# Two-part SwiGLU input products in 512 columns, a new order of the mixers' pieces, and other loads and final norm

## The chip, the cores and the metric

The kernel runs on one core of a Trainium2 chip. The core has a matrix engine (TensorE; PE in the profile, PEld for its loading of weights), VectorE (DVE), ScalarE (ACT), GpSimd (POOL) and a queue engine (SP) that here only issues DMAs. Sixteen DMA engines move data between the chip's memory (HBM) and the core's own (SBUF); TensorE writes into PSUM, eight banks of 512 four-byte columns in each of 128 partitions. The metric is the device time of one execution in microseconds (us).

## What is computed

The reference is an encoder of two layers over 256 tokens of 1024 channels in float32. Each layer adds half a SwiGLU, a mixer of three kinds of heads, and half a second SwiGLU; a norm ends it.

```python
def rms_norm(x, g):
    xf = x.astype(jnp.float32)
    y = xf * lax.rsqrt(jnp.mean(xf * xf, axis=-1, keepdims=True) + EPS)
    return (y * g.astype(jnp.float32)).astype(x.dtype)

def swiglu(h, w_in, w_out):
    gate, up = jnp.split(h @ w_in, 2, axis=-1)
    return (jax.nn.silu(gate) * up) @ w_out
...
    for l in range(DEPTH):
        lam_init = 0.8 - 0.6 * math.exp(-0.3 * l)
        x = x + 0.5 * swiglu(rms_norm(x, ln_ffn1[l]), ffn1_w_in[l], ffn1_w_out[l])
        h = rms_norm(x, ln_mix[l])
        x = x + hybrid_mixer(h, w_mix_in[l], conv_w[l], sink_logits[l], diff_lambda[l],
                             diff_norm_g[l], dn_A_log[l], dn_dt_bias[l], dn_norm_g[l],
                             w_mix_out[l], lam_init)
        x = x + 0.5 * swiglu(rms_norm(x, ln_ffn2[l]), ffn2_w_in[l], ffn2_w_out[l])
    return rms_norm(x, ln_final)
```

The hidden width of SwiGLU is 2752. The mixer projects 1024 channels to windowed attention (6 heads), differential attention (4 heads) and a gated delta rule (6 heads, forward and backward, in chunks of 64 tokens, with a short convolution ahead of it and a triangular inverse for each chunk), and projects the joined heads back.

## The kernel before

**Layout.** x stays in SBUF through the whole kernel with channels on the partitions: `x[128, 8, 256]`, eight blocks k of 128 channels by 256 tokens. Weights come from HBM once, in tiles of 128x1024 (512 KB), through a ring of eight raw tiles `wr` (L255).

**Two-part products.** The SwiGLUs and the mixer's last projection split both operands into a high part, rounded to the matrix engine's fast four-byte type, and the rest. `load` (L257 on) writes the high part `wh` of a weight tile on ACT (L264) and the low part `wl` on DVE (L265); `prep` does the same for x times the norm's gain, giving `xh` (L243) and `xl` (L244). `mm3` (L270 to L272) then adds three products: high by high, high weight by low x, low weight by high x. Each is one weight load of 128x128 and one pass of 256 columns.

**SwiGLU** (`ffn`). The input stage runs over 21 blocks j of 128 hidden channels and a tail of 64. Gate and up of a block are 2 x 8 groups of `mm3`, and share one PSUM bank, 256 columns each (block 0 has two banks). `hidden` then multiplies the gate by the norm's factor `rb` (L288, DVE), takes its silu (L289, ACT), multiplies it by up (L291, DVE), and splits it into `hh` and `hl` (L293, ACT; L294, DVE). The output stage runs over 8 blocks d of output channels, 21 groups of `mm3` and a tail each, and adds to x on DVE (L360, L361). The norm's factor is computed after block 1 (`norm_scale`): sums of squares by products with a column of ones (L211), the root on DVE or ACT, and a product that spreads it over the partitions (L220).

**Start** (`start`). SP issues four loads of x, each followed by a quarter of the two weight tiles of block 0 (`ar`); ACT issues `cols`, the gains and conv weights. Block 0 runs as pieces arrive.

**Mixer** (`mixer`). Some 150 pieces (projections, conv taps, scores, softmaxes, rows of the inverse, scan steps, output products) are issued in the order of the string `ORDER`. A piece may be: `c` a conv channel block, `co` its silu and transposition, `p` an attention projection, `d` and `w` scores of a differential or windowed head, `h` and `hw` their outputs, `ir`, `im`, `io` parts of the inverse, `sa`, `sb`, `sc` parts of a scan step, `z` a gate projection, `o` an output product. `BANK` names the PSUM pool of each kind of product: `pm` has two banks, `pd` four, `pt` two. `SHARED` lists pieces of work that go to another engine than their usual one: `t` a conv tap through ACT and POOL, `g` a slope added by a matrix product instead of DVE (L710), `S` and `O` parts of the scan on POOL instead of DVE (L1033, L1046), `x` a residual addition on ACT and POOL (L1079, L1080), `s` a part of silu on POOL.

The Tile framework turns the program into one fixed instruction stream for each engine, and may move an instruction ahead of one that it expects to wait; the order of the program gives the priorities.

**End** (`final`). The final norm's factor stays in PSUM; eight DVE instructions (L1129) multiply x, gain and factor, 256 columns each, and four DMAs on two queues write pairs of blocks.

Of the kernel before, what the change touches and what calls it, by code (L numbers as in the profile page):

```python
# [56 lines left out]
class Kernel:  # L57
    def __init__(self, ctx, tc, ins, out):
# [12 lines left out]
        self.x = self.xp.tile([P, KD, S], F32, tag="x", name="x")  # L71
        self.col = cp.tile([P, 150], F32, name="col")
# [3 lines left out]
        warm = cp.tile([P, 1], F32, name="warm")  # L76
        nc.scalar.activation(warm, self.onec, AF.Copy)

    def start(self, gcol, pool=None, src=None):

        nc = self.nc
        n = KD // 2
        self.ahead = []
        if pool is not None:
            for j in range(2):
                w, go = self.fetch(src, j * 1024, 1024, n, pool)
                h = pool.tile([P, 1024], F32R, name=f"ah{j}")
                lo = pool.tile([P, 1024], F32R, name=f"al{j}")
                self.ahead.append((w, go, h, lo))
        for i in range(n):  # L90
            nc.sync.dma_start(self.x[:, 2 * i : 2 * i + 2, :], self.ins["x"][:, 2 * i : 2 * i + 2, :])
            for w, go, h, lo in self.ahead:
                go[i]()
            if i == 0:
                nc.scalar.dma_start(self.col, self.ins["cols"])
        for i in range(n):
            for k in (2 * i, 2 * i + 1):
                self.prep(k, gcol, False)
            c = slice(i * 256, i * 256 + 256)
            for w, go, h, lo in self.ahead:  # L100
                nc.scalar.activation(h[:, c], w[:, c], AF.Copy)
                nc.vector.tensor_tensor(lo[:, c], w[:, c], h[:, c].bitcast(F32), ALU.subtract)
        self.ahead = [a[2:] for a in self.ahead]
# [99 lines left out]

    def norm_scale(self, name, last=False, log=True):

        nc = self.nc
        ps = self.psum([P, 512], f"{name}_ps", "pt")
        for p in range(2):
            parts = [t for t in (self.sq, self.sq7) if t is not None]
            for t in parts:  # L210
                nc.tensor.matmul(  # L211
                    ps[:, p : p + 1], lhsT=t[:, p * P : (p + 1) * P], rhs=self.onec, start=t is parts[0], stop=t is parts[-1]
                )
        v = self.sp.tile([P, 2], F32, tag="nv", name=f"{name}_v")
# [52 lines left out]

    def mm3(self, out, ah, al, bh, bl, start, stop):
# [6 lines left out]
    def ffn(self, l, i, gnext, first, late=False):  # L275
# [3 lines left out]
        with tc.tile_pool(name=f"hp{nm}", bufs=1) as hp, tc.tile_pool(name=f"ht{nm}", bufs=3) as ht:  # L279
# [3 lines left out]

            def hidden(j, gate, up, rows, base):
                t = ht.tile([P, S], F32, tag="t", name="t")
                s = ht.tile([P, S], F32, tag="s", name="s")
                h = ht.tile([P, S], F32, tag="h", name="h")
                nc.vector.tensor_tensor(t[:rows], gate, rb[:rows], ALU.mult)  # L288
                nc.scalar.activation(s[:rows], t[:rows], AF.Silu)  # L289
# [57 lines left out]
            for d in range(KD):  # L347
# [940 lines left out]
```

## Time and profile before

| | us |
|---|---|
| median of 3 runs | 1120.86 (1120.8 to 1122.6) |
| the profiled execution's own time | 1121.32 |
| its span, first to last instruction | 1119.5 |
| mean granted TensorE clock, share of full | 0.991 |

The profile shows one execution. An instruction's row gives its line, engine, operation, output and inputs, shape and count. "Busy" is the time in which an engine has an instruction under way; matrix products overlap each other, so their mean duration (283 ns for 256 columns) is longer than the step from one to the next. "Idle before" names what ended an engine's wait. The stages, by their instructions: SwiGLU to 197 us, mixer to about 355, SwiGLUs to 747, the second mixer to 904, SwiGLU to 1109, final norm. A few per cent of the matrix products can be missing from such a record.

### The profile page before, as it was taken

To read this page: it belongs to the slowest core of one execution; us is meant where nothing else is said; L and a number is where in the kernel's file an instruction comes from. 1 tells how busy PE (TensorE), PEld (TensorE's weight loads), DVE (VectorE), ACT (ScalarE), POOL (GpSimd) and SP (SyncE) were. 2 spreads that over 40 slices of the span, in tenths; PEclk is the share of its full clock that TensorE was granted. 3 is DMA by queue.
4 is the path that set the end of the run, shared out by engine and by line. 5 is a ranking of instruction groups with operands and counts; after the bars stand their busy time and mean duration, and the time that the engine had idled before them with its cause. 6 is when DMAs were issued, how large, how long until landed. Compare 5 with 4: busy or idle time off the path is not lost.

```text
span 1119.5 us, 22207 instructions
## 1 busy us (share of the span) xinstructions
PE 1077.2 (96%) x9098; PEld 1009.7 (90%) x9098; DVE 751.0 (67%) x1374; ACT 545.4 (49%) x1006; POOL 60.1 (5%) x109
## 2 busy tenths in 40 slices
PE   7999999999799999999999999999989999999996
PEld 7999999777568999999999999988756789999996
DVE  7766654579958866666566666536897697666643
ACT  6544433263773654544444454423648455445441
POOL 0000001100101000000000000121010010000010
PEclk9999999999899999999999999999989999999998
DMA  9655654422322555565555565534223135555521
GB/s 331 225 182 187 199 178 136 132 94 95 113 96 77 165 174 189 182 200 184 171 174 184 188 197 182 170 115 150 85 85 132 42 130 172 189 183 195 187 95 38
DMA packets 49637, 173.65 MB, mean 155 GB/s; under 512 B 5504, under 2 KB 6784, under 8 KB 49536
## 3 DMA queue, kind: packets, MB, share of 16 engines
q1 hardware_dynamic: 49104, 171.64, 46.2%
q8 instruction: 71, 1.16, 0.4%
q10 hardware_dynamic: 432, 0.60, 0.2%
q14 instruction: 30, 0.25, 0.1%
HBM read 171.17 MB, written 1.05 MB: 154 GB/s over the span
## 4 chain that ended last, share of the span: by engine, by line
PE 78%; DVE 13%; ACT 4%; issue 3%; DMA 1%; POOL 1%; DVEq 0%; SPq 0%; ACTq 0%
PE ps L272 21%; PE ps L270 21%; PE ps L271 21%; PE pj L455 4%; PE pv L466 2%; DVE pr L825 2%; DVE wl L265 2%; PE py L270 1%; DVE pp L826 1%; PE py L271 1%; PE py L272 1%; DVE pad L568 1%; ACT wh L264 1%; DVE mxd L740 1%; PE px L995 1%
## 5 line engine op out<-in xcount | busy, mean ns | idle before, releaser
L265 DVE TENSOR_TENSOR wl<-wr,wh 128x1024 fp32r<-128x1024 f32 x270 | 330.5, 1226 | 167.6 <-ACT wh L264 167.1
L264 ACT ACTIVATE wh<-wr 128x1024 fp32r<-128x1024 f32 x270 | 284.2, 1054 | 243.9 <-issue 153.0
L270 PE MATMUL ps<-xh,wh 128*128 128x256 f32 x1336 | 378.6, 283 | 0.6 <-ACT wh L264 0.6
L272 PE MATMUL ps<-xh,wl 128*128 128x256 f32 x1336 | 378.3, 283 | 0.8 <-DVE wl L265 0.8
L271 PE MATMUL ps<-xl,wh 128*128 128x256 f32 x1336 | 377.9, 283 | 0.0
L272 PEld LDWEIGHTS ps<-xh,wl 128*128 128x128 f32 x1336 | 256.3, 192 | 1.2 <-DVE wl L265 1.2
L270 PEld LDWEIGHTS ps<-xh,wh 128*128 128x128 f32 x1336 | 256.3, 192 | 0.8 <-ACT wh L264 0.8
L271 PEld LDWEIGHTS ps<-xl,wh 128*128 128x128 f32 x1336 | 256.3, 192 | 0.0
L270 PE MATMUL ps<-hh,wh 128*128 128x256 f32 x672 | 190.2, 283 | 0.0
L271 PE MATMUL ps<-hl,wh 128*128 128x256 f32 x672 | 190.2, 283 | 0.0
L272 PE MATMUL ps<-hh,wl 128*128 128x256 f32 x672 | 190.2, 283 | 0.0
L455 PE MATMUL pj<-xf,wr 128*128 128x256 f32 x544 | 128.8, 387 | 1.2 <-DVE dqk L686 1.2
L270 PEld LDWEIGHTS ps<-hh,wh 128*128 128x128 f32 x672 | 129.0, 192 | 0.0
L271 PEld LDWEIGHTS ps<-hl,wh 128*128 128x128 f32 x672 | 129.0, 192 | 0.0
L272 PEld LDWEIGHTS ps<-hh,wl 128*128 128x128 f32 x672 | 129.0, 192 | 0.0
L455 PEld LDWEIGHTS pj<-xf,wr 128*128 128x128 f32 x544 | 101.7, 193 | 18.3 <-issue 3.9
L293 ACT ACTIVATE hh<-h 128x256 fp32r<-128x256 f32 x88 | 36.1, 416 | 90.3 <-DVE h L291 90.3
L198 POOL TENSOR_TENSOR sqacc<-sqacc,sqt 128x256 f32<-128x256 f32 x27 | 24.5, 907 | 741.6 <-ACT sqt L194 741.6
L288 DVE TENSOR_TENSOR t<-ps,f_rb 128x256 f32<-128x256 f32 x88 | 36.9, 424 | 38.0 <-PE ps L272 37.7
L294 DVE TENSOR_TENSOR hl<-h,hh 128x256 fp32r<-128x256 f32 x88 | 36.8, 423 | 30.4 <-ACT hh L293 30.4
L194 ACT ACTIVATE sqt<-x 128x256 f32<-128x256 f32 x49 | 19.8, 409 | 56.3 <-DVE x L361 52.5
L568 DVE SCALAR_TENSOR_TENSOR pad<-pad,cwh 128x256 f32<-128x256 f32 x68 | 33.1, 487 | 12.1 <-ACT pad L562 6.8
(319 smaller groups left out, 1212.7 us busy)
## 6 DMA issues: line engine op xcount, KB each, us to landing
wr<-in_ffn SPq DMA_DIRECT2D x258, 512.0 KB, 3.4
wr<-in_mix SPq DMA_DIRECT2D x50, 512.0 KB, 3.4
wr<-in_mix SPq DMA_DIRECT2D x8, 408.0 KB, 3.1
wr<-in_mix SPq DMA_DIRECT2D x8, 384.0 KB, 2.9
x<-in_x SPq DMA_DIRECT2D x4, 256.0 KB, 4.1
ar<-in_ffn SPq DMA_DIRECT2D x8, 128.0 KB, 4.2
cb<-in_constb SPq DMA_DIRECT2D x1, 588.0 KB, 10.2
out_y<-fo SPq DMA_DIRECT2D x2, 256.0 KB, 2.4
```

The source lines that it names most:

```text
L198: (eng or nc.gpsimd).tensor_tensor(self.sq, self.sq, t, ALU.add)
L264: nc.scalar.activation(h, w, AF.Copy)
L265: nc.vector.tensor_tensor(lo, w, h.bitcast(F32), ALU.subtract)
L270: mm(out, lhsT=ah, rhs=bh, start=start, stop=False)
L271: mm(out, lhsT=ah, rhs=bl, start=False, stop=False)
L272: mm(out, lhsT=al, rhs=bh, start=False, stop=stop)
L288: nc.vector.tensor_tensor(t[:rows], gate, rb[:rows], ALU.mult)
L293: nc.scalar.activation(hh[:n, j, :], h[:n], AF.Copy)
L294: nc.vector.tensor_tensor(hl[:n, j, :], h[:n], hh[:n, j, :].bitcast(F32), ALU.subtract)
L455: mm(ps[:, 0:S], lhsT=w[:, k * P : (k + 1) * P], rhs=xf[:, k, :], start=k == 0, stop=k == KD - 1)
L466: mm(st[name][p][:, 0:n], lhsT=xf[:, k, p * P : (p + 1) * P], rhs=w[:, c], start=k == 0, stop=k == KD - 1)
L568: stt(cv, pad[:, w : w + S], cw[:, i * 5 + w : i * 5 + w + 1], cv, ALU.mult, ALU.add)
```

## The change

Five things change together.

1. In the input stage of SwiGLU, high and low part of x stand side by side in a tile `x2` (`[128, 2, 256]` for each k). `mm2` multiplies the high weight by both at once, 512 columns into a whole PSUM bank, and the low weight by the high part, 256 columns into the bank's first half. `halves` copies the second half out (ACT) and adds the first (DVE). Gate and up have a bank each in every block. The output stage and the mixer keep `mm3`. In block 0 the weights are packed so that the first tile holds k 0 to 3 of gate and up.
2. At the start, x and `cols` lie in one array that ACT's queue loads in three pieces; the weights of block 0 go over SP in two pieces and one whole tile; six products of zeros run on PE before.
3. The order of the mixers' pieces, some PSUM pools and some of the sharing between engines are others.
4. In the final norm, x times the gain is written by ACT during the last output stage (`xg`); DVE multiplies by the factor in four instructions of 512 columns.
5. Around the last norm's sums, twice three products without use (`idle_mm`) run on PE.

```diff
-lt A:0 A:1 A:2 K N A:3 G V c:1:0 c:1:1 c:0:0 c:0:2 c:1:2 clear GS co:1:0 c:0:1 co:1:1 co:1:2 ce:1 GE GT E:1 qn:1
-co:0:0 co:0:1 co:0:2 ce:0 qn:0 qc:1:1 E:0 E:3 qc:1:0 c:2:0 c:2:1 E:2 qc:0:0 qc:0:1 ic X:0:0 X:1:1 X:0:1 X:1:0 i ir:1:2
-ir:2:3 ir:3:4 ir:4:5 ir:5:6 p:15 ir:6:7 ir:7:8 im:0 im:1 im:2 c:2:2 p:14 p:13 co:2:0 p:16 d:0 d:2 co:2:1 co:2:2 im:3
...
+lt K A:0 A:1 clear A:2 N A:3 V c:0:0 c:1:0 c:1:1 c:1:2 G c:0:2 co:1:0 co:1:1 c:0:1 co:1:2 co:0:0 c:2:1 GS ce:1 GT qn:1
+qc:1:0 GE co:0:1 co:0:2 E:1 ce:0 qn:0 qc:0:1 E:0 qc:0:0 qc:1:1 E:3 ic X:0:0 X:0:1 c:2:0 E:2 X:1:1 X:1:0 i ir:1:2
+ir:2:3 ir:3:4 p:14 ir:4:5 ir:5:6 ir:6:7 ir:7:8 p:15 im:0 p:13 im:1 co:2:0 im:2 p:16 im:3 co:2:1 c:2:2 d:2 d:1 p:12
...
-    pj="pm", pv="pd", pz="pm", py="pm", pss="pd", pg="pt", pgr="pd", ptr="pd", pkq="pt", pe="pd", pq="pd", p1="pd",
-    p2="pt", pk="pd", px="pt", pS="pt", po="pd", pw="pt", pT="pd", pso="pd", pto="pd",
+    pj="pm", pv="pd", pz="pm", py="pm", pss="pd", pg="pt", pgr="pd", ptr="pd", pkq="pt", pe="pd", pq="pt", p1="pt",
+    p2="pt", pk="pd", px="pt", pS="pt", po="pt", pw="pt", pT="pd", pso="pt", pto="pt",
...
-SHARED = set("O2 d0 d1 d2 d3 g5 s3 t1 t8 x4 x5 x6".split())
+SHARED = set("O3 S1 d0 d1 d2 d3 g2 g5 s4 t0 t3 t8 x0 x4 x6 x7".split())
...
+            zero = pool.tile([P, S], F32, name="zero")
+            nc.vector.memset(zero, 0.0)
+            wm = self.psum([P, 512], "wm", "pt")
+            for i in range(NWARM):
+                nc.tensor.matmul(wm[:, 0:S], lhsT=zero[:, 0:P], rhs=zero, start=True, stop=True)
             for j in range(2):
-                w, go = self.fetch(src, j * 1024, 1024, n, pool)
+                w, g = self.fetch(src, j * 1024, 1024, 2 - j, pool)
+                go += g
...
-        for i in range(n):
-            nc.sync.dma_start(self.x[:, 2 * i : 2 * i + 2, :], self.ins["x"][:, 2 * i : 2 * i + 2, :])
-            for w, go, h, lo in self.ahead:
-                go[i]()
-            if i == 0:
-                nc.scalar.dma_start(self.col, self.ins["cols"])
+        cuts = [0] + [NCOL + 512 * i for i in (1, 2, 4)]
+        for a, b in zip(cuts, cuts[1:]):
+            nc.scalar.dma_start(self.xc[:, a:b], self.ins["x"][:, a:b])
+        warm = self.cp.tile([P, 1], F32, name="warm")
+        nc.scalar.activation(warm, self.onec, AF.Copy)
+        for g in go:
+            g()
...
+    def mm2(self, bank, ah, al, b, start, stop):
+
+        mm = self.nc.tensor.matmul
+        mm(bank, lhsT=ah, rhs=b.rearrange("p a t -> p (a t)"), start=start, stop=False)
+        mm(bank[:, 0:S], lhsT=al, rhs=b[:, 0, :], start=False, stop=stop)
...
+            def halves(ps, tag):
+
+                u = ht.tile([P, S], F32, tag=tag, name=tag)
+                nc.scalar.activation(u, ps[:, S : 2 * S], AF.Copy)
+                nc.vector.tensor_tensor(u, u, ps[:, 0:S], ALU.add)
+                return u
...
-                nc.vector.tensor_tensor(t[:rows], gate, rb[:rows], ALU.mult)
-                nc.scalar.activation(s[:rows], t[:rows], AF.Silu)
+                nc.vector.tensor_tensor(gate, gate, rb[:rows], ALU.mult)
+                nc.scalar.activation(s[:rows], gate, AF.Silu)
...
-                ps = self.psum([P, 512], "ps", "pm" if j % 3 == 0 else "pd")
-                pu = self.psum([P, 512], "pu") if j == 0 else ps
+                ps, pu = (self.psum([P, 512], t, "pm" if j % 3 == 0 else "pd") for t in ("ps", "pu"))
...
-                    self.mm3(o, w[g][0][:, c], w[g][1][:, c], self.xh[:, k, :], self.xl[:, k, :], k == 0, k == KD - 1)
+
+                    n, q = (k // 4, k // 2 % 2 * 4 + g * 2 + k % 2) if j == 0 else (g, k)
+                    c = slice(q * P, (q + 1) * P)
+                    self.mm2((ps, pu)[g], w[n][0][:, c], w[n][1][:, c], self.x2[k], k == 0, k == KD - 1)
...
-                        hidden(j_, pg[:, 0:S], pu[:, S : 2 * S], P, (0,))
+                        hidden(j_, halves(pg, "t"), halves(pu, "u"), P, (0,))
...
                 if gnext is None:
                     self.sq_add(d, last=d == KD - 1)
+                    if d == 0:
+                        self.xg = self.xp.tile([P, KD, S], F32, tag="xh", name="xg")
+                    nc.scalar.activation(self.xg[:, d, :], self.x[:, d, :], AF.Copy, scale=self.col[:, 48 + d : 49 + d])
...
-        for k in range(KD):
-            nc.vector.scalar_tensor_tensor(o[:, k, :], self.x[:, k, :], self.col[:, 48 + k : 49 + k], rb, ALU.mult, ALU.mult)
-            if k % 2:
-                (nc.sync, nc.scalar)[k // 2 % 2].dma_start(self.out[:, k - 1 : k + 1, :], o[:, k - 1 : k + 1, :])
+        for i in range(KD // 2):
+            k = slice(2 * i, 2 * i + 2)
+            nc.vector.tensor_tensor(o[:, k, :], self.xg[:, k, :], rb.unsqueeze(1).to_broadcast([P, 2, S]), ALU.mult)
+            (nc.sync, nc.scalar)[i % 2].dma_start(self.out[:, k, :], o[:, k, :])
```

`idle_mm(3)` runs the products of 256 columns with the identity as weight, once ahead of the sums of the last norm and once behind them.

More of the change, by code (lines that the diff above doesn't have):

```diff
@@ L32 @@
 NROW = 158
+NCOL = 150
+NWARM = 6
 C_U0, C_U1, C_ONE, C_ID, C_MM = 0, 128, 256, 384, 512
@@ L70, in __init__ @@
         cp = self.cp
-        self.x = self.xp.tile([P, KD, S], F32, tag="x", name="x")
-        self.col = cp.tile([P, 150], F32, name="col")
+        self.xc = self.xp.tile([P, NCOL + KD * S], F32, tag="x", name="x")
+        self.col = self.xc[:, 0:NCOL]
+        self.x = self.xc[:, NCOL:].rearrange("p (k t) -> p k t", k=KD)
         self.cst = None
@@ L98, in start @@
                 self.prep(k, gcol, False)
-            c = slice(i * 256, i * 256 + 256)
-            for w, go, h, lo in self.ahead:
+            if self.ahead:
+                w, h, lo = self.ahead[i // 2]
+                c = slice(i % 2 * 512, i % 2 * 512 + 512)
                 nc.scalar.activation(h[:, c], w[:, c], AF.Copy)
                 nc.vector.tensor_tensor(lo[:, c], w[:, c], h[:, c].bitcast(F32), ALU.subtract)
-        self.ahead = [a[2:] for a in self.ahead]
+        self.ahead = [a[1:] for a in self.ahead]
     def constants(self):
@@ L202, in log_table, with idle_mm @@
         self.tc.keep_in_program_order(self.nc.scalar.preload_act_table_set("natural_log_exp_and_others"))
+    def idle_mm(self, n, tag="pm"):
+        ps = self.psum([P, 512], "idle", tag)
+        for i in range(n):
+            self.nc.tensor.matmul(ps[:, 0:S], lhsT=self.ident, rhs=self.cst[:, C_U0 : C_U0 + S], start=True, stop=True)
     def norm_scale(self, name, last=False, log=True):
         nc = self.nc
+        if last:
+            self.idle_mm(3)
         ps = self.psum([P, 512], f"{name}_ps", "pt")
@@ L213, in norm_scale @@
                 )
+        if last:
+            self.idle_mm(3)
         v = self.sp.tile([P, 2], F32, tag="nv", name=f"{name}_v")
@@ L239, in prep @@
         if k == 0:
-            self.xh = self.xp.tile([P, KD, S], F32R, tag="xh", name="xh")
-            self.xl = self.xp.tile([P, KD, S], F32R, tag="xl", name="xl")
+            self.x2 = []
+        if k % 4 == 0:
+            x2 = self.xp.tile([P, KD // 2, 2, S], F32R, tag=("xh", "xl")[k // 4], name="x2")
+            self.x2 += [x2[:, i] for i in range(KD // 2)]
         g = self.col[:, gcol + k : gcol + k + 1]
-        nc.scalar.activation(self.xh[:, k, :], self.x[:, k, :], AF.Copy, scale=g)
+        nc.scalar.activation(self.x2[k][:, 0, :], self.x[:, k, :], AF.Copy, scale=g)
         nc.vector.scalar_tensor_tensor(
-            self.xl[:, k, :], self.x[:, k, :], g, self.xh[:, k, :].bitcast(F32), ALU.mult, ALU.subtract
+            self.x2[k][:, 1, :], self.x[:, k, :], g, self.x2[k][:, 0, :].bitcast(F32), ALU.mult, ALU.subtract
         )
@@ L331, in ffn @@
                 c = slice(k * P, (k + 1) * P)
-                self.mm3(ps[:, 0:S], wh[:, c], wl[:, c], self.xh[:, k, :], self.xl[:, k, :], k == 0, k == KD - 1)
-            hidden(NF, ps[0:TAIL, 0:S], ps[TAIL : 2 * TAIL, 0:S], TAIL, (0, TAIL))
+                self.mm2(ps, wh[:, c], wl[:, c], self.x2[k], k == 0, k == KD - 1)
+            t = halves(ps, "t")
+            up = ht.tile([P, S], F32, tag="u", name="up")
+            nc.scalar.activation(up[:TAIL], t[TAIL : 2 * TAIL], AF.Copy)
+            hidden(NF, t[:TAIL], up[:TAIL], TAIL, (0, TAIL))
             if gnext is None:
@@ L1254, in pack @@
     gh = np.stack([np.tile(f[n][l], 2) for l in range(DEPTH) for n in ("diff_norm_g", "dn_norm_g")], axis=1)
-    out["cols"] = np.concatenate([g.transpose(2, 0, 1).reshape(P, 56), cw, gh], axis=1)
+    cols = np.concatenate([g.transpose(2, 0, 1).reshape(P, 56), cw, gh], axis=1)
+    out["x"] = np.concatenate([cols, out["x"].reshape(P, KD * S)], axis=1)
     rows = [
```

21 lines of the change are left out of this document (10 added, 11 removed).

## The prediction

> **What bounds the kernel now.** I read the page first: engine shares, then the chain that ended last.
>
> ```profile
> span 1119.5 us, 22207 instructions
> PE 1077.2 (96%) x9098; PEld 1009.7 (90%) x9098; DVE 751.0 (67%) x1374; ACT 545.4 (49%) x1006; POOL 60.1 (5%) x109
> PE ps L272 21%; PE ps L270 21%; PE ps L271 21%; PE pj L455 4%; PE pv L466 2%; DVE pr L825 2%; DVE wl L265 2%; PE py L270 1%; DVE pp L826 1%; PE py L271 1%; PE py L272 1%; DVE pad L568 1%; ACT wh L264 1%; DVE mxd L740 1%; PE px L995 1%
> ```
>
> TensorE is the bound, and 63% of the chain is the three products of SwiGLU. Next, the windows by stage (columns: length, then busy time and count of PE, PEld, DVE, ACT, POOL, clock, DMA):
>
> ```profile
> 0.00:5.80 5.80, 0.00 (x0) 0.00 (x0) 1.19 (x8) 2.69 (x6) 0.51 (x12) 1.00 0.61 187
> 5.80:13.80 8.00, 7.94 (x48) 7.88 (x48) 7.40 (x21) 7.19 (x22) 0.00 (x0) 1.00 0.97 316
> 13.80:30.00 16.20, 14.77 (x118) 14.04 (x117) 14.36 (x36) 9.54 (x10) 0.00 (x0) 1.00 1.02 400
> 58.00:138.00 80.00, 80.00 (x669) 80.00 (x668) 52.13 (x73) 39.04 (x58) 0.00 (x0) 1.00 0.58 191
> 197.50:355.00 157.50, 146.59 (x1307) 114.43 (x1307) 122.20 (x294) 84.97 (x226) 15.31 (x29) 0.98 0.31 101
> 746.70:904.00 157.30, 146.70 (x1306) 114.41 (x1306) 121.93 (x293) 84.78 (x226) 15.24 (x29) 0.98 0.31 101
> ```
>
> In the SwiGLU stage PE has no gap: 669 products in 80.0 us, 119.6 ns each. A mixer leaves PE idle for 157.5 - 146.6 = 10.9 us. So the first question is what sets the 119.6 ns.
>
> **SwiGLU input.** Three products of 256 columns become one of 512 and one of 256: weight loads fall from three to two, columns stay at 768. The count is 4 x (21 x 16 + 8) = 1376 groups; the page shows 1336 under one name, the rest have other tile names. What a group costs depends on which of the two, columns or loads, sets the pace. These rows (start, duration; the last one is a tile's minimum, median, maximum in ns) separate them:
>
> ```profile
> 7.22 0.41 PE L272 MATMUL pu<-xh,al 128*128 128x256 f32 x1
> 9.35 0.41 PE L270 MATMUL pu<-xh,ah 128*128 128x256 f32 x1
> 209.69 17.28 PE pj L455 x80
> 266.41 0.59 PE L732 MATMUL pss<-ddb,sdiag 128*128 128x512 bf16 x2
> L732 PE MATMUL pss<-ddb,sdiag x16: 379/379/379, 266.4 to 828.2; 128*128 128x512 bf16 x16
> 300.18 1.10 PE L784 MATMUL pso<-V,PT 128*128 128x64 f32 x8
> L784 PE MATMUL pso<-V,PT x64: 275/275/323, 293.3 to 858.4; 128*128 128x64 f32 x64
> ```
>
> In the slow first microseconds the same products stand 10 steps apart over 2.13 us: 213 ns. [...] A product of only 64 columns with a four-byte 128x128 weight still takes (1.10 - 0.275) / 7 = 118 ns. So about 118 to 120 ns is the floor of a **weight load**, whatever is streamed. Two bf16 products of 512 columns take 0.59, one 0.379: 211 ns. [...] So I price the 512-column product at 216 and the 256-column one behind it at 120 ns: 336 for 360, **24 ns a group, 1376 x 24 = 33.0 us**. [...]
>
> [...]
>
> What the halves cost: per block of 128 hidden channels, two ACT copies out of PSUM and two DVE additions. From the stage's groups (58 to 138 us; the third column is idle time before them):
>
> ```profile
> L265 DVE TENSOR_TENSOR wl<-wr,wh 128x1024 fp32r<-128x1024 f32 x28 | 34.3, 1225 | 14.4 <-ACT wh L264 14.4
> L264 ACT ACTIVATE wh<-wr 128x1024 fp32r<-128x1024 f32 x28 | 29.4, 1051 | 22.1 <-issue 22.1
> L288 DVE TENSOR_TENSOR t<-ps,f_rb 128x256 f32<-128x256 f32 x14 | 6.0, 425 | 7.2 <-PE ps L272 7.2
> L294 DVE TENSOR_TENSOR hl<-h,hh 128x256 fp32r<-128x256 f32 x14 | 5.9, 424 | 5.8 <-ACT hh L293 5.8
> L293 ACT ACTIVATE hh<-h 128x256 fp32r<-128x256 f32 x14 | 5.8, 417 | 17.6 <-DVE h L291 17.6
> L291 DVE TENSOR_TENSOR h<-s,ps 128x256 f32<-128x256 f32 x14 | 5.8, 415 | 0.0
> L289 ACT ACTIVATE s<-t 128x256 f32<-128x256 f32 x14 | 5.6, 399 | 0.0
> L1079 ACT ACTIVATE xt<-py x6: 363/377/384, 355.3 to 909.0; 128x256 f32<-128x256 f32 x6
> ```
>
> DVE per block: 2 x 1.225 + 0.425 + 0.415 + 0.424 = 3.71 us, plus 2 x 0.42 = 4.55. ACT: 2 x 1.051 + 0.399 + 0.417 = 2.92, plus 2 x 0.377 = 3.67. The block itself goes from 16 x 0.36 = 5.76 to 16 x 0.336 = 5.38. Both fit, so I cost them at **0**; DVE stands at 85% then. Each block takes two PSUM banks instead of one, so three blocks are in flight; at the start block 3 waits for block 0's banks, but the halves are read out before the norm's factor is known. The weight stream rises from 191 to some 205 GB/s, far under the 400 that the start shows: 0. The new packing of block 0 asks for the second tile earlier; in later SwiGLUs both are loaded ahead: 0.
>
> **Start.** Loads go out on two queues, weights in 3 pieces instead of 8, and six zero products run before the data.
>
> ```profile
> 0.73 0.42 ACTq L95 DMA_DIRECT2D col<-in_cols  x1
> 1.18 1.28 ACT L77 ACT_TABLE_LOAD   x1 [1.18 <-PEq L1276]
> 5.86 0.58 PE L270 MATMUL ps<-xh,ah 128*128 128x256 f32 x1 [5.86 <-ACT ah L101]
> 10.03 0.42 ACT L101 ACTIVATE ah<-ar 128x256 fp32r<-128x256 f32 x1 [0.48 <-DMA ar<-in_ffn]
> 14.61 0.38 PE L270 MATMUL ps<-xh,wh 128*128 128x256 f32 x1 [0.61 <-ACT wh L264]
> 15.87 0.39 PE L272 MATMUL ps<-xh,wl 128*128 128x256 f32 x1 [0.76 <-DVE wl L265]
> ```
>
> Block 0 waits for its last piece of weights at 10.0 us, and its first 20-odd products run at 213 instead of 120 ns: 2 us. Earlier pieces and a warm array are worth 0 to 3 us together. What follows is close to DMA and DVE (1.02 and 14.36 of 16.2 us busy), where the additions go too, so I take **2 us**. On ACT's queue three loads of x now stand ahead of the table load: 3 x 0.42 + 1.28 from 0.73 us on ends at 3.3, before the first product at 5.9, so 0. [...]
>
> **Mixers.** The pieces are the same; their order, some PSUM pools and the sharing between engines differ. Two windows, one wait in the timeline, and the prices of what changes engine (L1033: minimum, median, maximum):
>
> ```profile
> 270.00:285.00 15.00, 10.44 (x56) 7.47 (x56) 14.93 (x21) 8.44 (x29) 2.54 (x2) 0.95 0.22 71
> 285.00:300.00 15.00, 12.60 (x64) 10.15 (x64) 13.98 (x22) 9.00 (x22) 3.55 (x2) 0.82 0.45 141
> 286.21 2.17 PE L699 MATMUL pss<-wq 64*128 64x256 f32 x8 [5.77 <-DVE c L748]
> 294.99 0.69 DVE L710 SCALAR_TENSOR_TENSOR sc<-wd,pss 128x512 f32<-128x512 bf16 x1 [0.35 <-PE pT L436]
> L1033 DVE TENSOR_TENSOR Stmp<-SC,egl x6: 551/554/557, 333.0 to 888.1; 64x384 f32<-64x384 f32 x4, 128x384 f32<-128x384 f32 x2
> L568 DVE SCALAR_TENSOR_TENSOR pad<-pad,cwh 128x256 f32<-128x256 f32 x68 | 33.1, 487 | 12.1 <-ACT pad L562 6.8 <-POOL pad L566 3.1 <-POOL pad L552 0.3
> 343.25 1.02 POOL L1046 TENSOR_TENSOR O<-O,SC 128x384 f32<-128x384 f32 x1 [44.53 <-DVE SC L1044]
> ```
>
> Most of PE's idle time lies between 270 and 300 us, where DVE runs the inverse and is 96% busy; one PE wait there is 5.77 us. DVE is relieved of one slope addition (0.69), one conv tap net (0.49), the scaling of the state in scan step 1 (2 x 0.55) and one residual addition (0.42): 2.7 us, of which only the slope stands near the full stage. POOL takes those at about 1 us each and has time; the two state halves end before the product that they meet, so 0. Five tiles move from a pool of four banks to one of two, and may make products wait. What the new order is worth isn't visible in a trace of the old one: at best the idle 10.9 us, at worst another wait of the size of that 5.77. I take 2 us a mixer, near the relief: **4 us**, bounds +22 and -12.
>
> **End.** Multiplying by the gain moves into the last stage; then come 4 products of 512 columns instead of 8 of 256.
>
> ```profile
> 1110.13 0.38 PE L211 MATMUL fin_ps<-onec,sqt 128*128 128x1 f32 x2 [1.37 <-ACT sqt L194]
> 1112.27 0.71 PE L220 MATMUL fin_pb<-cst,fin_r 128*128 128x128 f32 x4 [1.31 <-DVE fin_r L182]
> 1113.02 3.22 DVE L1129 SCALAR_TENSOR_TENSOR fo<-x,col,fin_pb 128x256 f32<-128x256 f32 x8 [0.81 <-PE fin_pb L220]
> ```
>
> A 512-element DVE pass is 0.69: about 2.5 for 3.22, **0.7 us**. The idle products, 3 x 0.216 us, fit into PE's 1.37 and 1.31 us waits; uncovered they would cost 0.65 each. The added ACT pass lies beside the norm chain: 0.
>
> **Sum.** The profiled execution took 1121.3 us (span 1119.5 and 1.8 around it). 1121.3 - 33.0 - 2.0 - 4.0 - 0.7 = 1081.6; the median of the runs, 1120.9, lies 0.4 lower: **1081 us**.
>
> **Rivals.**
> [...]
> - *Columns set the pace.* No gain from the groups: 1121.3 - 6.7 = 1114.6, less than 0.6% faster. [...]
> - *DVE becomes the bound, slower.* Its waits for ACT in the stage were (14.4 + 5.8) / 14 = 1.44 us a block. If in the new fixed order none of them hides behind other work, a block takes 4.55 + 1.44 = 5.99 us, 0.23 more than 5.76: 84 blocks x 0.23 = 19 us, 1121.3 + 19 - 6.7 = 1134. It costs from 5.38 us a block on and makes the kernel slower from 5.76 + 6.7 / 84 = 5.84. Against it: DVE can run ahead by two pairs of weight tiles, and waits shrink when it is late.
>
> **Chances.** Forecast 0.70, exchange cost 0.13, columns 0.07, DVE 0.10 (0.07 of it beyond the break-even). A measurement of this kernel can tell about 0.2% from no change. Faster: 0.70 + 0.13 + 0.06 + 0.02 = 0.91; same 0.02; slower 0.07. The range 1066 to 1100 takes in the forecast with the mixers 15 us better or 12 worse, and the exchange cost, about 0.8.
>
> **What would show it.** In the stage's windows PE without gaps and 16 groups in 5.38 us, the 512-column products 216 ns from the next, the others 120 (227 and 120 for the exchange cost, 240 and 120 for columns); DVE near 85% and idle only on PE. Wrong if PE shows idle time for DVE or ACT in the SwiGLU stage, if a mixer is longer than 157 us, or if block 1 does not start before 14.6 us.

## The result, and the profile after

The changed kernel takes **1111.6 us** (median of 4 runs, 1110.03 to 1112.02), the kernel before 1121.62 beside it. The ratio is 0.9905, 95% interval 0.9893 to 0.9917: faster by 10 us, 0.95%, where 40 us were forecast. The profiled execution took 1112.02 us; the sum of the prediction, 1081.6, is 30.4 us below it.

From the page of the changed kernel: its span, TensorE's share, and the chain that ended last by line.

```profile
span 1110.2 us, 19882 instructions
PE 1074.5 (97%) x7746; PEld 937.5 (84%) x7748; DVE 797.4 (72%) x1529; ACT 597.9 (54%) x1190; POOL 70.0 (6%) x117
PE ps L296 15%; PE pu L296 14%; PE ps L297 7%; PE pu L297 7%; PE ps L302 7%; PE ps L303 7%; PE ps L301 7%; PE pj L498 5%; DVE pr L868 2%; PE pv L509 2%; PE py L301 1%; PE py L302 1%; DVE wl L290 1%; PE py L303 1%; ACT kq L669 1%
```

1352 products fewer, and TensorE is busy only 2.7 us less (1077.2 before). L296 is the new 512-column product, L297 the 256-column one behind it. A window of the changed kernel in the SwiGLU input (columns as in the prediction):

```profile
400.00:480.00 80.00, 80.00 (x459) 69.77 (x458) 62.71 (x102) 47.34 (x87) 0.00 (x0) 1.00 0.59 195
```

TensorE has no gap there, as before. The 459 products make 229.5 groups, 348.6 ns each. The timeline of one gate tile shows the two products apart (start, duration with its modelled end):

```profile
59.63 0.39 PE L296 MATMUL ps<-x,wh 128*128 128x512 f32 x1
59.86 0.28 PE L297 MATMUL ps<-x,wl 128*128 128x256 f32 x1
59.98 0.39 PE L296 MATMUL ps<-x,wh 128*128 128x512 f32 x1
...
62.31 0.28 PE L297 MATMUL ps<-x,wl 128*128 128x256 f32 x1
62.43 0.39 PE L296 MATMUL pu<-x,wh 128*128 128x512 f32 x1
```

Eight groups lie between 59.63 and 62.43: 350 ns each, 233 to 235 for 512 columns and 115 to 120 for 256. Forecast were 216 + 120 = 336.

Four marks cut both executions into the same stages: the first value projection of each mixer (`pv`) and the sums of the norm behind it (`f_ps`). Before, then after:

```profile
197.57 2.90 PE L466 MATMUL pv<-wr,xf 128*128 128x408 f32 x8
383.28 0.50 PE L211 MATMUL f_ps<-onec,sqacc 128*128 128x1 f32 x4
746.77 8.38 PE L466 MATMUL pv<-wr,xf 128*128 128x408 f32 x24
932.47 0.50 PE L211 MATMUL f_ps<-onec,sqacc 128*128 128x1 f32 x4
```

```profile
192.29 8.04 PE L509 MATMUL pv<-wr,xf 128*128 128x408 f32 x23
380.49 0.50 PE L231 MATMUL f_ps<-onec,sqacc 128*128 128x1 f32 x4
737.74 8.38 PE L509 MATMUL pv<-wr,xf 128*128 128x408 f32 x24
926.26 0.50 PE L231 MATMUL f_ps<-onec,sqacc 128*128 128x1 f32 x4
```

| stage | before | after | difference |
|---|---|---|---|
| to the first mixer | 197.57 | 192.29 | -5.28 |
| mixer 1 and two SwiGLU blocks | 185.71 | 188.20 | +2.49 |
| SwiGLUs between the mixers | 363.49 | 357.25 | -6.24 |
| mixer 2 and two SwiGLU blocks | 185.70 | 188.52 | +2.82 |
| the rest of the last SwiGLU, final norm | 187.03 | 183.94 | -3.09 |
| span | 1119.5 | 1110.2 | -9.3 |

The SwiGLU stages gain some 13 of the 33 us forecast, and each mixer is longer instead of shorter. At the end of the kernel, after:

```profile
1103.24 0.52 PEld L242 LDWEIGHTS fin_pb<-cst,fin_r 128*128 128x128 f32 x4 [0.74 <-DVE fin_r L194]
1103.99 2.48 DVE L1174 TENSOR_TENSOR fo<-xg,fin_pb 128x512 f32<-128x512 f32 x4 [0.80 <-PE fin_pb L242]
```

The last pass is 2.48 for 3.22 us, as forecast. But from its end to the end of the span 3.73 us pass (1110.2 - 1106.47) where it was 3.26 before, and TensorE runs idle products between the norm's sums: the pass starts 4.84 us after SwiGLU's last product (1099.15) where it was 4.66 (1108.36 to 1113.02).

### The profile page after: what moved, and what is told of

It is laid out like the page before. It is cut to its first block, busy times and chain, and to the rows that moved or that the text cites. A ratio compares the mean times of both kernels' runs of the same rounds, so it can differ in the third digit from the quotient of the medians.

```text
span 1110.2 us, 19882 instructions
## 1 busy us (share of the span) xinstructions
PE 1074.5 (97%) x7746; PEld 937.5 (84%) x7748; DVE 797.4 (72%) x1529; ACT 597.9 (54%) x1190; POOL 70.0 (6%) x117
## 4 chain that ended last, share of the span: by engine, by line
PE 80%; DVE 11%; ACT 5%; issue 2%; DMA 1%; POOL 0%; ACTq 0%; DVEq 0%
PE ps L296 15%; PE pu L296 14%; PE ps L297 7%; PE pu L297 7%; PE ps L302 7%; PE ps L303 7%; PE ps L301 7%; PE pj L498 5%; DVE pr L868 2%; PE pv L509 2%; PE py L301 1%; PE py L302 1%; DVE wl L290 1%; PE py L303 1%; ACT kq L669 1%
## 5 line engine op out<-in xcount | busy, mean ns | idle before, releaser
L289 ACT ACTIVATE wh<-wr 128x1024 fp32r<-128x1024 f32 x270 | 285.9, 1059 | 276.2 <-issue 185.9
L296 PE MATMUL ps<-x,wh 128*128 128x512 f32 x696 | 247.7, 393 | 0.0
L296 PE MATMUL pu<-x,wh 128*128 128x512 f32 x664 | 236.6, 393 | 0.0
L297 PE MATMUL ps<-x,wl 128*128 128x256 f32 x696 | 194.4, 279 | 0.0
L302 PE MATMUL ps<-hl,wh 128*128 128x256 f32 x672 | 189.8, 282 | 0.0
L297 PE MATMUL pu<-x,wl 128*128 128x256 f32 x664 | 185.3, 279 | 0.0
L296 PEld LDWEIGHTS ps<-x,wh 128*128 128x128 f32 x696 | 130.4, 187 | 30.5
L296 PEld LDWEIGHTS pu<-x,wh 128*128 128x128 f32 x664 | 124.4, 187 | 29.4
L297 PEld LDWEIGHTS ps<-x,wl 128*128 128x128 f32 x696 | 130.4, 187 | 0.2
L302 PEld LDWEIGHTS ps<-hl,wh 128*128 128x128 f32 x672 | 126.1, 188 | 0.0
L297 PEld LDWEIGHTS pu<-x,wl 128*128 128x128 f32 x664 | 124.4, 187 | 0.0
L328 DVE TENSOR_TENSOR h<-s,u 128x256 f32<-128x256 f32 x84 | 35.2, 423 | 9.1 <-ACT s L326 2.4
```

Source lines behind the costliest of these rows:

```text
L289: nc.scalar.activation(h, w, AF.Copy)
L296: mm(bank, lhsT=ah, rhs=b.rearrange("p a t -> p (a t)"), start=start, stop=False)
L297: mm(bank[:, 0:S], lhsT=al, rhs=b[:, 0, :], start=False, stop=stop)
L302: mm(out, lhsT=ah, rhs=bl, start=False, stop=False)
L328: nc.vector.tensor_tensor(h[b : b + rows], s[:rows], up, ALU.mult)
```

## Experiments

All are variants of the changed kernel unless the text says otherwise. "Alone" in a time means one run.

### What a product of the SwiGLU input costs

**The low-weight product over 512 columns** (adds the product of the two low parts).

```diff
-        mm(bank[:, 0:S], lhsT=al, rhs=b[:, 0, :], start=False, stop=stop)
+        mm(bank, lhsT=al, rhs=b.rearrange("p a t -> p (a t)"), start=False, stop=stop)
```

> The changed kernel with the low weight's product over 512 columns instead of 256 (it adds the low-by-low term). Now a group takes 349 ns, the steps in it 235 and 114. Load floor, as forecast (a 512-column product steps by 216): 2 x 216 = 432 ns a group, 1376 x 83 ns = 114 us more. [...] Columns alone (349 / 768 each): 465 ns, 160 us more.

Measured: 1271.87 us alone, 160.3 more, or 116.5 ns for each of 1376 groups. Its timeline:

```profile
69.68 0.40 PE L296 MATMUL ps<-x,wh 128*128 128x512 f32 x1
69.92 0.39 PE L297 MATMUL ps<-x,wl 128*128 128x512 f32 x1
...
71.78 0.40 PE L297 MATMUL ps<-x,wl 128*128 128x512 f32 x1
```

Nine steps in 2.10 us are 233.3 ns a product, 0.4557 ns a column. At that pace 768 columns take 350.0 ns, which is the group of the changed kernel with nothing left over. "Columns" holds for the changed group: two such products take 467 ns here, where columns asked for 465 and the load floor for 432.

**The low-weight product over 64 columns, and over 128** (the rest of this correction is left out).

```diff
-        mm(bank[:, 0:S], lhsT=al, rhs=b[:, 0, :], start=False, stop=stop)
+        mm(bank[:, 0:64], lhsT=al, rhs=b[:, 0, 0:64], start=False, stop=stop)
```

> The changed kernel with the low weight's product over the first 64 tokens only (its correction is left out for the other 192). With 128 tokens a group took 345 ns, only 4 less than with 256. If a weight load of some 112 to 118 ns is the floor there, 64 tokens take the same 345 ns. If a product in this type under 256 columns runs in two passes, the second product falls from 112 to about 58 and the group to 290 ns. Columns alone at 0.455 ns: 233 + 29 = 262 ns.

> The changed kernel with the low weight's product over the first 128 tokens only; the correction by the low part of the weights is left out for the other 128. Load floor: no product under 118 ns, so the group stays at 235 + 118 = 353 or falls to 216 + 118 = 334 ns. [...] Columns alone: 349 x 640 / 768 = 291 ns. [...]

With 64 columns: 1103.09 us alone.

```profile
59.57 0.48 PE L296 MATMUL ps<-x,wh 128*128 128x512 f32 x1
59.88 0.19 PE L297 MATMUL ps<-x,wl 128*128 128x64 f32 x1
59.91 0.48 PE L296 MATMUL ps<-x,wh 128*128 128x512 f32 x1
...
60.95 0.48 PE L296 MATMUL ps<-x,wh 128*128 128x512 f32 x1
```

The group is (60.95 - 59.57) / 4 = 345 ns, though 576 columns at 0.4557 would be 262. By difference the second product costs 345 - 233 = 112 ns with a quarter of its columns, though the time is lost ahead of it: it starts 310 to 320 ns after the 512-column product, and the next one 30 ns behind it. So the pair has a floor, and a wait for its two weight loads, the **load floor** of the prediction, fits; no run separates it from another floor. With 256 columns, which take 117 ns, it doesn't show. With 128 columns the group inside a tile is 345 ns as well, but the kernel takes 1215.47 us, slower. Its groups by what ended the idle time before them (58 to 130 us):

```profile
L297 PE MATMUL ps<-x,wl 128*128 128x128 f32 x88 | 20.6, 234 | 4.0 <-DVE wl L290 4.0
L297 PE MATMUL pu<-x,wl 128*128 128x128 f32 x83 | 19.4, 233 | 3.8 <-DVE wl L290 3.8
```

TensorE waits for weights split on DVE, 7.8 us in 72. DVE's fixed order came out otherwise for 128 columns (for 64 it is that of the changed kernel), so the time of this kernel says nothing on the product, only the group does.

**Both parts of x zero ahead of the SwiGLUs** (their results are left out).

```diff
-        nc.scalar.activation(self.x2[k][:, 0, :], self.x[:, k, :], AF.Copy, scale=g)
+        nc.scalar.activation(self.x2[k][:, 0, :], self.x[:, k, :], AF.Copy, scale=0.0)
-            self.x2[k][:, 1, :], self.x[:, k, :], g, self.x2[k][:, 0, :].bitcast(F32), ALU.mult, ALU.subtract
+            self.x2[k][:, 1, :], self.x[:, k, :], 0.0, self.x2[k][:, 0, :].bitcast(F32), ALU.mult, ALU.subtract
```

> The changed kernel with both parts of x set to zero ahead of every SwiGLU (so that these add nothing; the mixers work on x as it then is). If a product of 512 columns takes 233 ns instead of some 213 because of what the data make the array draw, it falls to 213 to 216 ns and a group from 349 to some 325. If it is a property of this type of product, whatever the data, it stays at 233 and 349 ns.

1113.83 us alone, and the same 459 products in the window from 400 to 480 us:

```profile
400.00:480.00 80.00, 80.00 (x459) 69.87 (x459) 62.39 (x101) 48.27 (x88) 0.00 (x0) 1.00 0.59 196
```

With x zero the pace is the same, 459 products in 80.00 us, so it doesn't hang on the values of x.

### The mixers: which part of the plan

The plan is ORDER, BANK and SHARED. Two kernels exchange it as a whole: the changed one with the old plan, and the one before with the new plan.

```diff
-ORDER, BANK, SHARED of the changed kernel
+ORDER, BANK, SHARED of the kernel before
```

> The changed kernel with the order of the mixers' pieces, the PSUM pools and the sharing of before. If these cost what the traces say (3.0 us in each mixer), 1111.6 - 6 = 1105.6 us. If the mixers are longer because of something else in the change (another phase of the weight stream, the blocks before and behind them), it stays at 1111 to 1112. If the new plan gains as I forecast, 1115.

> The kernel before with the new order, pools and sharing, and nothing else of the change. If the plan alone costs 3.0 us a mixer, 1121.6 + 6 = 1127.6 us; if it only loses beside the new SwiGLU, 1121.6; if it gains as I forecast, 1117.6.

The changed kernel with the old plan takes 1106.59 us (ratio to before 0.9864, 0.9849 to 0.9879), 5.0 less than with its own. The kernel before with the new plan takes 1129.39 (1.0063, 1.0042 to 1.0084). So the new plan costs 5 to 8 us, and the rest of the change gains 15.

Then each part alone goes back, and two of them together (old BANK and SHARED, new ORDER):

> The changed kernel with the old order of pieces; the pools and the sharing stay new. All three together cost 2.4 us in each mixer's stage (first product of pv to the next norm's sums: 188.2 us, 185.9 with all three old). If the order is the cause, the stage falls to 185.9 and the time to 1106.6 us; if the pools or the sharing are, it stays at 188.2 and 1111.6.

> The changed kernel with the old PSUM pools only. If five more kinds of tile in the pool of two banks make products wait, the stage falls to 185.9 us and the time to 1106.6; if order or sharing are the cause, 188.2 and 1111.6.

> The changed kernel with the old sharing between engines only. If the taps and additions that went to ScalarE and GpSimd come late, the stage falls to 185.9 us and the time to 1106.6. If the relief of VectorE was worth what I put on it, about 1 us a mixer, the stage rises to some 189 and the time to 1113.6.

> The changed kernel with the old pools and the old sharing, so that of the new plan only the order is left. The new pools cost 5.4 us and the new sharing 1.3 beside the others. If they add up, 1111.6 - 5.4 - 1.3 = 1105 us, 1.7 below the old plan; if the sharing only cost because of the pools, 1106.2.

And single tiles of BANK, in the changed kernel:

```diff
-    p2="pt", pk="pd", px="pt", pS="pt", po="pt", pw="pt", pT="pd", pso="pt", pto="pt",
+    p2="pt", pk="pd", px="pt", pS="pt", po="pd", pw="pt", pT="pd", pso="pt", pto="pt",
```

> The changed kernel with one entry of the pools back: po, the scan's product of queries and state, in the pool of four banks. In the changed kernel step 1's po waits until 335.5 us of the span, with the old pools it runs at 330.4. If that is what delays the scan, most of the old pools' 5.4 us comes back: 1107 us. If another of the five moved tiles does it, 1111.

> The changed kernel with pso (head outputs) and pto (transposed outputs) back in the pool of four banks. A mixer's stage less what it loses to clock dips (1.7 us each) is 186.7 us in the changed kernel and 184.9 with all five moved tiles back. If head outputs and scan tiles wait for each other in the small pool, it falls to 185; if not, it stays at 186.7.

> The changed kernel with pq (products of keys and queries, ahead of the inverse) back in the pool of four banks. If the inverse starts late because pq waits for banks of the small pool, the stage less dips falls from 186.7 to about 185 us; if the cause lies in the scan, it stays at 186.7.

The table has the median, the ratio to before with its interval, the two mixer stages by the marks above, and what the granted clock took from each: the sum over windows of 10 us of (1 - clock) x length.

| kernel | us | ratio | mixers | clock loss | mixers less loss |
|---|---|---|---|---|---|
| before | 1121.62 | | 185.7, 185.7 | 3.4, 3.5 | 182.3, 182.2 |
| changed | 1111.60 | 0.9905 (0.9893-0.9917) | 188.2, 188.5 | 1.7, 1.7 | 186.5, 186.8 |
| old plan | 1106.59 | 0.9864 (0.9849-0.9879) | 185.9, 186.0 | 3.4, 3.4 | 182.5, 182.6 |
| old ORDER | 1117.40 | 0.9959 (0.9939-0.9978) | 192.2, 188.6 | 8.5, 3.4 | 183.7, 185.2 |
| old BANK | 1106.24 | 0.9865 (0.9846-0.9883) | 187.0, 184.4 | 1.7, 0 | 185.3, 184.4 |
| old SHARED | 1110.34 | 0.9897 (0.9881-0.9914) | 187.7, 187.3 | 1.7, 1.7 | 186.0, 185.6 |
| old BANK, SHARED | 1109.29 | 0.9875 (0.9856-0.9895) | 185.1, 188.1 | 0, 3.4 | 185.1, 184.7 |
| `po` in pd | 1113.47 | 0.9916 (0.99-0.9933) | 187.0, 188.8 | 0, 1.7 | 187.0, 187.1 |
| `pso`, `pto` in pd | 1114.13 | 0.9932 (0.9916-0.9948) | 190.6, 189.2 | 3.5, 1.7 | 187.1, 187.5 |
| `pq` in pd | 1110.88 | 0.9903 (0.9887-0.992) | 189.0, 188.2 | 3.4, 1.7 | 185.6, 186.5 |

With the old ORDER alone the kernel is slower, which neither value of its expectation has: the mixers' work falls, but the clock takes 8.5 and 3.4 us.

Two things lie in it. **First, the clock.** The losses are steps of 1.7 us, and the two mixers of one execution, the same instructions, can differ by them: old BANK and SHARED, mixer 1 and mixer 2 (its windows):

```profile
192.35:377.45 185.10, 173.55 (x1489) 137.22 (x1488) 144.75 (x338) 102.91 (x261) 18.43 (x40) 1.00 0.32 107
734.71:922.78 188.07, 176.65 (x1489) 139.33 (x1488) 145.09 (x338) 102.97 (x261) 18.64 (x32) 0.98 0.32 105
```

Same 1489 products, 3.1 us more busy time, and two such steps. The changed kernel has one in each mixer (for each the window ahead of the step and the step itself, then the timeline's row at the first):

```profile
249.88:253.29 3.41, 1.08 (x6) 0.75 (x5) 3.35 (x5) 2.15 (x4) 0.00 (x0) 1.00 0.37 115
253.29:256.70 3.41, 3.41 (x10) 2.70 (x9) 2.94 (x16) 0.00 (x0) 0.00 (x0) 0.50 0.00 0
813.08:816.49 3.41, 3.03 (x11) 1.71 (x11) 3.36 (x8) 2.04 (x8) 0.00 (x0) 1.00 0.00 0
816.49:819.90 3.41, 3.41 (x10) 2.62 (x10) 2.23 (x6) 2.46 (x10) 2.06 (x1) 0.50 0.00 0
252.46 5.41 PE L498 MATMUL pj<-xf,wr 128*128 128x256 f32 x16 [2.33 <-DVE dqk L729]
```

In the first, TensorE waits 2.33 us for a PSUM bank that DVE reads late, and then runs 3.41 us at a clock of 0.50, which loses 1.7. Ahead of the second it was busy for 3.03 of 3.41 us, so a long wait isn't needed, and what starts a step stays open. Executions of one kernel differ by such steps, so single mixers are compared less their loss. But the level is largely the kernel's own: the mean granted clock is 0.990 or 0.991 in the executions of the kernel before and 0.995 to 0.997 in the four of the changed one. Two steps fewer (3.4 us by the table) are part of the 10 us that it gains. (A step that fell into a wait would cost less than 1.7, and the last column would then be too low; that is not shown by itself.)

**Second, the plan.** Less the clock, the new plan lengthens a mixer by some 4.2 us; one step of the clock fewer leaves +2.5. The old order brings 1.6 to 2.8 of it, old pools 1.2 to 2.4, old sharing 0.5 to 1.2; the new order alone costs 2.1 to 2.6 over the old plan. All executions together say the same: the median of time less span x (1 - mean granted clock), good to about 1 us, is 1106.3 for the changed kernel, 1097.8 with the old plan, 1101.3 with the old ORDER, 1103.8 with the old BANK and 1105.0 with the old SHARED. Of the pools no tile tried alone brings the gain back. That `po` waits in the changed kernel was the first suspect; moved, it starts 6.3 us earlier, of which 2.0 are this mixer's earlier start (191.96 for 192.29) and the clock step that it lacks (changed, then moved):

```profile
335.50 0.27 PE L1038 MATMUL po<-SC,kq 64*64 64x64 f32 x2
```

```profile
329.21 0.22 PE L1038 MATMUL po<-SC,kq 64*64 64x64 f32 x1
```

Yet the mixer, less its loss, isn't shorter. Which tiles together make up the pools' part stays open, and `p1` was not tried.

### A cost that is there and costs nothing

The differential scores are products of 32 rows (`dqk`). In every kernel with the new order, two heads a mixer have their records as 4 and 4 with the second bank's slope product between; in the old plan all have 8. Old plan, then changed:

```profile
264.45 1.13 PE L780 MATMUL pss<-dqk 32*128 32x256 f32 x8
265.51 2.86 PE L498 MATMUL pj<-xf,wr 128*128 128x256 f32 x12
```

```profile
269.61 0.38 PE L775 MATMUL pss<-ddb,sdiag 128*128 128x512 bf16 x1 [0.98 <-ACT sc L786]
269.92 1.13 PE L780 MATMUL pss<-dqk 32*128 32x256 f32 x4
270.98 0.39 PE L775 MATMUL pss<-ddb,sdiag 128*128 128x512 bf16 x1
271.30 1.12 PE L780 MATMUL pss<-dqk 32*128 32x256 f32 x4
```

Eight take 1.06 us to the next start, and so do four (269.92 to 270.98): 2 x 1.06 = 2.1 us a mixer, half of the 4.2. To undo it, the pieces were put apart, in the changed kernel and in the best one (below):

```diff
-... c:2:2 d:2 d:1 p:12
-io:0 d:3 co:2:2 h:2 p:9 io:1 d:0 w:0 ...
+... c:2:2 d:2 p:12
+io:0 co:2:2 d:1 h:2 p:9 d:3 io:1 d:0 w:0 ...
```

> The changed kernel with the pieces d:1, d:3 and d:0 (scores of the differential heads) put further apart in the order, so that the two score banks of each head are free together. Theory 'row groups': each product of these scores fills only 32 of the 128 rows, and the two maps of a head lie on different rows; in the traces of the old order their 8 records follow one another as 8 and take 1.06 us a head, in the new order two heads a mixer have them as 4 and 4, and each 4 takes 1.06 us. With all heads as 8 the records' own time falls from 6.35 to 4.3 us a mixer, and the mixer, less its clock losses, from 186.5 or more to 184.5: about 1107.5 us. Rival 'hidden': the DVE is what this stretch waits for, so TensorE only waits 2 us more behind them; mixer and time stay at 186.5 and 1111.6. Second rival 'order': moving d:1, d:3 and d:0 later costs more elsewhere than it gains; mixer above 187.

> The same edit of the order in the kernel with old pools and 512-column output products (1101.01 us). Row groups: each mixer 2 us shorter, 1097. Hidden: 1101. Order: above 1102.

Measured: 1117.31 us (0.9958, 0.9944 to 0.9971) and 1107.46 (0.9865, 0.9852 to 0.9879), both some 6 us slower. The records did what they should, all heads have 8:

```profile
263.76 1.13 PE L780 MATMUL pss<-dqk 32*128 32x256 f32 x8
269.47 1.13 PE L780 MATMUL pss<-dqk 32*128 32x256 f32 x8
278.98 1.13 PE L780 MATMUL pss<-dqk 32*128 32x256 f32 x8
280.58 1.13 PE L780 MATMUL pss<-dqk 32*128 32x256 f32 x8
```

But the mixers of the first take 189.8 and 192.0 with 3.4 and 5.1 lost to the clock: 186.4 and 186.9 without, as in the changed kernel (186.5 and 186.8). By the work "hidden" holds, by the time the rival "order": TensorE waits more instead (13.7 and 13.9 us idle for 12.7 and 13.0). The 6 us are three more steps of the clock (3.4 + 5.1 for 1.7 + 1.7, 5.1 us) and little else. They aren't chance: all five executions have a clock of 0.989 to 0.992, the four of the changed kernel 0.995 to 0.997. In the second, the mixers less loss are 185.2 and 184.8 for 184.3 and 184.3, with the same three steps more. So the split into 4 and 4 isn't what the new order costs; that stays open.

In the old plan, the four score products of a head were run map by map:

```diff
-                for p in range(2):
-                    for m in range(2):
+                for m in range(2):
+                    for p in range(2):
```

> The changed kernel with the old plan (1106.59 us, its mixers 185.9 us with 3.4 us of clock loss), in which the four score products of each head run map by map instead of alternating between the maps: same products, same banks, only the order of four neighbours. Row groups: the 8 records of a head take 1.8 to 2.1 us instead of 1.06, the records' own time rises from 4.32 to 7.5 or more a mixer, and the mixer less its clock losses from 182.5 towards 185.5, 1112. Hidden: the records' own time rises, the idle time of TensorE behind them falls by as much, and the mixer stays at 182.5, 1106.6. If the records' own time does not rise at all, the 4 and 4 cost something else (the bank or the slope product between them), and row groups fall.

1106.8 us (0.9864, 0.985 to 0.9877), the same as the old plan, and the records still take 1.07:

```profile
264.36 1.14 PE L780 MATMUL pss<-dqk 32*128 32x256 f32 x8
265.43 2.86 PE L498 MATMUL pj<-xf,wr 128*128 128x256 f32 x12
```

So alternation isn't what makes 8 as short as 4, and by the letter of the expectation the theory of row groups falls. What is left is the slope product on all 128 rows between the two lots (270.98 us above); its part was not tried by itself.

### Start

The kernel with the old BANK, without the zero products:

```diff
-NWARM = 6
+NWARM = 0
```

> The changed kernel with the old pools and without the six products of zeros at the start; 1106.2 us with them. If they are what gains at the start, block 0 runs its first products at 213 ns per 256 columns again, and the first product of the mixer (192.1 us with them) comes up to 2 us later; if the loads are what gains, it stays at 192.1 and 1106.2.

1108.48 us (0.989, 0.9865 to 0.9915) for 1106.24; the first mixer begins at 193.32 instead of 192.13. Start of block 0 without them, and in the changed kernel with them:

```profile
8.26 0.63 PE L296 MATMUL ps<-x,ah 128*128 128x512 f32 x1
8.69 0.41 PE L297 MATMUL ps<-x,al 128*128 128x256 f32 x1
8.90 0.63 PE L296 MATMUL pu<-x,ah 128*128 128x512 f32 x1
```

```profile
7.71 0.40 PE L296 MATMUL ps<-x,ah 128*128 128x512 f32 x1
7.94 0.28 PE L297 MATMUL ps<-x,al 128*128 128x256 f32 x1
8.06 0.39 PE L296 MATMUL pu<-x,ah 128*128 128x512 f32 x1
...
10.75 0.50 PE L296 MATMUL ps<-x,ah 128*128 128x512 f32 x1 [0.78 <-DVE x L269]
...
13.94 0.39 PE L296 MATMUL ps<-x,wh 128*128 128x512 f32 x1
```

A group is 0.64 us without and 0.35 with them. They are worth 1.2 us by the start of the mixer; up to 10.75 the array waits 0.78 us for DVE's low part of x, which takes back a part of the head start.

### A version that beats both

The old BANK, and the SwiGLU output product built like the input: `hh` and `hl` side by side, one 512-column and one 256-column product a group, the halves added behind.

```diff
-            hh = hp.tile([P, NF + 1, S], F32R, name="hh")
-            hl = hp.tile([P, NF + 1, S], F32R, name="hl")
+            h2 = hp.tile([P, NF + 1, 2, S], F32R, name="h2")
+            hh, hl = h2[:, :, 0, :], h2[:, :, 1, :]
...
-self.mm3(o, cur[0][:, c], cur[1][:, c], hh[:, f, :], hl[:, f, :], f == 0, False)
+self.mm2(ps, cur[0][:, c], cur[1][:, c], h2[:, f], f == 0, False)
...
-nc.tensor.matmul(o, lhsT=th[:, c], rhs=hh[:, NF, :], start=False, stop=False)
-nc.tensor.matmul(o, lhsT=th[:, c], rhs=hl[:, NF, :], start=False, stop=True)
+nc.tensor.matmul(ps, lhsT=th[:, c], rhs=h2[:, NF].rearrange("p a t -> p (a t)"), start=False, stop=True)
+t = halves(ps, "t")
```

> The changed kernel with the old PSUM pools, and SwiGLU's output products in the form of its input products (both parts of the hidden channels side by side, 512 columns by the high weight, 256 by the low one, the halves added behind). If three products of 256 columns pay 358.8 ns and the two 349, the gain is 672 x 9.8 = 6.6 us less some 0.8 for the halves behind the last block: 1106.2 - 5.8 = 1100.4 us. If the gain of the input products came from something else (the banks, the earlier start), it stays at 1106.

**1101.01 us** (1099.56 to 1101.55; 0.9803, 0.979 to 0.9817). The output stage, old BANK alone and then with it:

```profile
138.00:188.00 50.00, 49.95 (x417) 49.88 (x417) 26.62 (x37) 18.21 (x22) 5.75 (x6) 1.00 0.49 161
138.00:188.00 50.00, 50.00 (x285) 43.51 (x285) 30.07 (x43) 20.50 (x29) 7.30 (x6) 1.00 0.51 160
```

139 groups become 142.5 in the same 50 us, 351 ns for 360. Over 672 groups that is 6 us; 5.2 came. So the two-product form gains the same in a second place, without the input stage's other changes. The old plan with this output stage was not run.

## Why the prediction was wrong

- **TensorE is the bound, no gaps in SwiGLU: right.** So were the covers: DVE stands at 62.71 / 80.00 = 78% (85% forecast), and the rival in which it becomes the bound doesn't show in the changed kernel. Something like it shows in the 128-column variant, where DVE's order differs and TensorE waits for the split weights: the splits, two a block, start at 70.27, 73.72 and 77.17 us, which is 6.90 us a block, for 5.60 in the changed kernel. The pace of the changed input stage is that of its columns (768 x 0.4557 = 350 ns a group).
- **The failed step is "So I price the 512-column product at 216".** The rows for it were a bf16 product of 512 columns (211) and the projections, 256 columns a record (17.28 / 80 = 216), which are other types; no run shows 216 ns for a 512-column product of the SwiGLU's type. The SwiGLU's own fast four-byte type took 0.4557 ns a column, 233 ns for 512. With 117 behind it the group is 350 for 360 ns, not 336. The marks give the difference more finely: 6.24 us for the 656 groups between the mixers are 9.5 ns, 3.0 for the 312 of the last stage 9.7. At 9.7 it is 1376 x 9.7 = **13.3 us instead of 33.0**. This is 20 of the 30 us.
- **The inference that led there** read the 119.6 and the 118 ns as a load floor. In the changed kernel 256 columns take 117 ns: columns and floor (112) lie 5 ns apart there, and the 118 ns row of the mixer couldn't separate them. The "columns" rival had the law right up to 3 ns a product of 256 columns, (359 - 350) / 3, which go with the new form; they are the whole gain. What takes them isn't shown. Loads follow each other without a gap there (PEld 80.00 of 80.00 us, 69.77 after), so a wait for loads, the prediction's floor at 119.6, fits. No run shows the "exchange cost" of the chances (227 and 120 ns): 512 columns stepped at 233 ns, and two such products took 467, 0.4557 a column with nothing left over. The total came nearest to "columns" (1114.6), and that is luck: it leaves out 13.3 us of gain in the groups and has the mixers 9.3 us too short.
- **Mixers: 4 us gained were forecast, with the wrong sign.** They took 5.3 more by the marks (+2.49 and +2.82), some 6 without the SwiGLU blocks in these stages, and 8.8 less the clock's steps. The failed step is "I take 2 us a mixer, near the relief". The relief was worth nothing: beside the new order and pools, the old sharing, which has none of it, makes a mixer 0.5 to 1.2 us shorter less the clock, and beside the old pools the two sharings are level (185.1 and 184.7 for 185.3 and 184.4). The new order and pools make it longer. The bound of -12 held it. This is 10 of the 30 us. How order and pools make it longer stays open.
- **Start: right.** Forecast 2.0; the first stage is 5.28 shorter, of which 344 groups x 9.7 ns = 3.3 are SwiGLU's: 2.0. Not all of it lies in block 0: block 1 starts at 13.94, not 14.61, 0.67 us earlier, and behind it TensorE had 0.82 us without work up to 30 us before, and none after. The six zero products took 4.27 us and ended 1.16 us before block 0's first product at 6.64; a group of block 0 behind them takes 0.35 us, 0.64 without them.
- **End: the pass right (0.74 for 0.7), the sum not.** 0.1 us came, since the landing took 0.47 longer and the pass started 0.18 later (4.84 for 4.66), where the sums waited beside the idle products.

## What to carry to other kernels

Take a product's price per column from a row of the same type, not from another type of the same width (512 columns took 233 ns here, 211 in bf16), and look for a second row at another width before a pace is called a load floor. Before an engine's relief is priced, show that the wait that it ends is the last one: 2.7 us a mixer on DVE brought nothing here. Shorter work on TensorE in a stretch that waits for DVE came back as idle time (13.7 and 13.9 us a mixer for 12.7 and 13.0). Before two versions of a stage are compared, take out the clock's steps, or compare many executions; but steps that every execution of a version has are part of its cost.

## What was not expected of the hardware

- The fast four-byte type streamed at 0.4557 ns a column (233.3 ns for 512), and with x zero the changed kernel kept its pace, 459 products in 80.00 us. Without the zero products a group takes 640 ns in the first microseconds and 350 later, a factor of 1.83. Two other rows of the kernel are a bf16 product of 512 columns with 211 ns and a record of the plain float32 projections, 256 columns, with 216.
- A 512-column product and a short one behind it took 345 ns with 64 columns and with 128, and 350 with 256.
- The granted clock stood at 0.50 for 3.41 us at a time, 1.7 us lost each (253.29 to 256.70 and 816.49 to 819.90 us above); the mixers had between none and five such steps, and the same mixer in the same program had none in one layer and two in the next. TensorE was partly busy ahead of both steps, 1.08 and 3.03 of 3.41 us.
- Eight records of products on 32 rows, for two maps on different rows, take 1.06 us, and so do four, for one map, when a product on all rows stands between the two lots.
